# The second feed-forward product of a transformer block by Strassen's seven block products in seven of eight groups, with the gate product and the weight sums on GpSimd

## The chip, the cores and the metric

The kernel runs on one core of a Trainium2 chip. The core has five engines that run beside each other and meet at semaphores: TensorE (PE in the profile; its weight loads are PEld), VectorE (DVE), ScalarE (ACT), GpSimd (POOL) and SyncE (SP), which issues most of the DMAs. Operands lie in SBUF, products of TensorE land in eight PSUM banks of 128 x 512 float32. The metric is the device time of one execution in microseconds (us); the median of three runs of the kernel before is 1342.85 us.

## The reference, cut to what matters

One layer of a hybrid block on 512 latent tokens of width 1024. The part that matters here is its end, the feed-forward network of hidden width 4096, its gate and the final norm:

```python
def _ffn(h, w1, w2):
    return jnp.square(jax.nn.relu(h @ w1)) @ w2
...
xl = xl + ga2_l * _ffn(_modulate(_rmsnorm(xl, norm2_g[l]), sh2_l, sc2_l), w_ff1[l], w_ff2[l])
...
return _rmsnorm(xl, final_g)
```

Everything is float32. `h @ w1` is 512 x 1024 by 1024 x 4096, the second product 512 x 4096 by 4096 x 1024.

## The kernel before

TensorE multiplies in a rounded float32 type (`F32R`). To keep precision every operand is split into a rounded part and a remainder, hi and lo, and every product is three matmuls, hi·hi, hi·lo and lo·hi (`mm3`, L105 to L108). A split is a ScalarE cast (hi) and a VectorE subtraction (lo): `split` (L110 to L112) for activations, `wpiece` (L91 to L103) for a 128 x 1024 piece of weights, which it also loads over SP's queue into one of three buffers (`wraw`).

The feed-forward part begins at L911. Its 4096 hidden units are 32 tiles of 128, in eight groups of four. For a group g:

- `w1load` loads and splits the four pieces of w1 (L918), `ff1` multiplies them with the normed activations `h2T` (24 matmuls of 128 x 128 by 128 x 512 a tile, L942), and ScalarE and VectorE make relu, square and split of the result (L944 to L947): the tile `fT`, hidden units by tokens.
- `w2load` loads the four pieces of w2 (L955), VectorE multiplies them by the gate row `ga2` (L956), ScalarE casts (L958), VectorE subtracts (L963).
- `ff2` multiplies: for each of four token tiles t and two column halves n, four hidden tiles by three matmuls go into one PSUM bank (L977), and VectorE adds the bank to the residual `x1[t]` (L978). In the last group the final norm and the output follow (L979 to L998).

The loop at L1001 issues `ff1(g)`, then `ff2(g-1)`, so TensorE always has a group's product in hand whose operands are a whole stage old. The gate row `ga2` is made by `row` (L772): a transpose on TensorE, a copy, a write to memory and a broadcast read of 128 x 1024.

The framework's scheduler sets the order on each engine when the program is built; each engine then works its list strictly in that order. A tile's buffer is given out again once its last reader is done, and a DMA that waits for a buffer holds up the rest of SP's list.

Of the kernel before, what the change touches and what calls it, by code (L numbers as in the profile page):

```python
# [13 lines left out]
P = 128  # L14
# [33 lines left out]
def block(ctx, tc, a, out):  # L48
# [622 lines left out]
    with ExitStack() as fs:  # L671
# [184 lines left out]
        def last_part(t, between=None):  # L856
            tt = slice(t * P, (t + 1) * P)
            for n in range(2):
                nn = slice(n * 512, (n + 1) * 512)
                for k in range(NP1, KT):  # L860
                    w = ws[k]
                    mm3(po[2 * t + n], (yT[k][:, 0, tt], yT[k][:, 1, tt]), (w[0][:, 0, nn], w[1][:, 0, nn]),
                        False, k == KT - 1)
                nc.vector.tensor_tensor(out=x1[t][:, nn], in0=po[2 * t + n], in1=x1[t][:, nn], op=ALU.add)
                nc.scalar.activation(out=po[2 * t + n], in_=x1[t][:, nn], func=AF.Square, scale=1.0 / 32.0,
                                     accum_out=sqs[t][:, n:n + 1])
                if n == 0 and between:
# [47 lines left out]
        def w1load(g):  # L915
            r = []
            for i in range(4):
                w = wpiece(a["w1"][4 * g + i], (KT, P))  # L918
                r.append([[w[p_][:, k, :] for k in range(KT)] for p_ in range(2)])
                mod(tlast[0])  # L920
            return r

        def ff1(g, ws):
            r = []
            pfs = []
            if g == 0:
# [8 lines left out]
            for i in range(4):
                w = ws[i]
                if g == 0:
                    pf = pfs[i]
                else:
                    pf = bank("pf")  # L940
                    for k in range(KT):
                        mm3(pf, (w[0][k], w[1][k]), (h2T[:, 0, k, :], h2T[:, 1, k, :]), k == 0, k == KT - 1)  # L942
                rl = t2("rl")
                nc.scalar.activation(out=rl, in_=pf, func=AF.Relu)  # L944
                nc.scalar.activation(out=rl, in_=rl, func=AF.Square)
                ft = h6([P, 2, T], F32R, "fT") if g % 2 == 0 else m4([P, 2, T], F32R, "fT")
# [4 lines left out]
        def w2load(g):  # L951
            r = []
            for i in range(4):
                raw = wraw("w2raw")
                nc.sync.dma_start(out=raw, in_=a["w2"][4 * g + i])  # L955
                nc.vector.tensor_tensor(out=raw, in0=raw, in1=ga2, op=ALU.mult)  # L956
                hi = m4([P, D], F32R, "w2h")
                nc.scalar.copy(out=hi, in_=raw)  # L958
                lo = []
                for n in range(2):  # L960
                    nn = slice(n * 512, (n + 1) * 512)
                    l_ = s2("w2l", F32R)
                    nc.vector.tensor_tensor(out=l_, in0=raw[:, nn], in1=hi[:, nn].bitcast(F32), op=ALU.subtract)  # L963
                    lo.append(l_)
                r.append((hi, lo))
            return r

        def ff2(g, ft, w2):
            for t in range(NT):
                tt = slice(t * P, (t + 1) * P)  # L970
                if g == NG - 1:
                    sq = m2p.tile([P, 4], F32, tag="ss", name="ss")
                for n in range(2):
                    nn = slice(n * 512, (n + 1) * 512)
                    pf = bank("pf2")
                    for i in range(4):
                        mm3(pf, (ft[i][:, 0, tt], ft[i][:, 1, tt]), (w2[i][0][:, nn], w2[i][1][n]), i == 0, i == 3)  # L977
                    nc.vector.tensor_tensor(out=x1[t][:, nn], in0=pf, in1=x1[t][:, nn], op=ALU.add)  # L978
# [9 lines left out]
                if g == NG - 1:
                    nc.scalar.activation(out=sq[:, 3:4], in_=sq[:, 1:2], func=AF.Sqrt, bias=sq[:, 2:3])
                    nc.vector.reciprocal(out=sq[:, 3:4], in_=sq[:, 3:4])  # L990
                    for n in range(2):
                        nn = slice(n * 512, (n + 1) * 512)
                        if n:
                            nc.scalar.activation(out=xo[:, nn], in_=xo[:, nn], func=AF.Copy, scale=sq[:, 3:4])
                        else:
                            nc.vector.tensor_scalar(out=xo[:, nn], in0=xo[:, nn], scalar1=sq[:, 3:4],
                                                    scalar2=None, op0=ALU.mult)
                        (nc.scalar if n else nc.sync).dma_start(out=out[t * P:(t + 1) * P, nn], in_=xo[:, nn])  # L998

        prev = None  # L1000
        for g in range(NG):  # L1001
            ft = ff1(g, w1)
            m_ = mlast[0]
            if g + 1 < NG:
                w1 = w1load(g + 1)
            if g == 0:
                ga2 = row(modc[:, 5, :], m1p.tile([P, D], F32, tag="r2", name="ga2"), m_)
            if prev is not None:
                ff2(*prev)
            w2 = w2load(g)  # L1010
            prev = (g, ft, w2)
        ff2(*prev)


def _layout(np, i):
# [43 lines left out]
    d["w2"] = x(f["w_ff2"][0].reshape(NFF, P, D))  # L1059
# [32 lines left out]
```

## Time and profile before

| what | value |
|---|---|
| three runs: lowest, median, highest | 1342.56, 1342.85, 1344.24 us |
| the profiled execution: time, span | 1341.42, 1339.7 us |
| granted TensorE clock | 0.999 |
| DMA over the span | 176.35 MB, mean 132 GB/s |
| feed-forward groups 1 to 7 in the trace | from about 1006 us to the end |

A page of the profile gives busy time by engine and groups instructions by line, engine and shape. A matmul's listed duration (about 390 ns) covers its whole way through the array; the next begins long before it ends, so the distance between starts is what counts. The windows view gives each engine's busy time in a stretch; the timeline gives starts and durations in order of time. "<-" ahead of an engine names what ended the idle time before an instruction.

### The profile page before, as it was taken

To read this page: it belongs to the slowest core of one execution; us is meant where nothing else is said; L and a number is where in the kernel's file an instruction comes from. 1 tells how busy PE (TensorE), PEld (TensorE's weight loads), DVE (VectorE), ACT (ScalarE), POOL (GpSimd) and SP (SyncE) were. 2 spreads that over 40 slices of the span, in tenths; PEclk is the share of its full clock that TensorE was granted. 3 is DMA by queue.
4 is the path that set the end of the run, shared out by engine and by line. 5 is a ranking of instruction groups with operands and counts; after the bars stand their busy time and mean duration, and the time that the engine had idled before them with its cause. 6 is when DMAs were issued, how large, how long until landed. Compare 5 with 4: busy or idle time off the path is not lost. (4 is left out here: it accounts for less than half of the span.)

```text
span 1339.7 us, 16566 instructions
## 1 busy us (share of the span) xinstructions
PE 1314.7 (98%) x6214; PEld 1095.2 (82%) x6214; DVE 949.5 (71%) x1480; ACT 591.1 (44%) x857; POOL 64.0 (5%) x223
## 2 busy tenths in 40 slices
PE   6999999999999999999999999999999999999997
PEld 4778888888888888888888878888898888888886
DVE  6777968599987796777998458866577454554536
ACT  4548663346362364523646255322345332342224
POOL 2000000000010000000000010100010000000000
PEclk9999999999999999999999999999999999999999
DMA  9794332322332223322234468865534321333102
GB/s 352 281 337 134 105 105 92 65 78 95 96 117 77 65 79 105 114 74 63 87 96 138 134 207 272 300 193 189 188 111 142 110 93 52 122 110 109 65 32 79
DMA packets 84068, 176.35 MB, mean 132 GB/s; under 512 B 31730, under 2 KB 38034, under 8 KB 83987
## 3 DMA queue, kind: packets, MB, share of 16 engines
q1 hardware_dynamic: 78802, 157.46, 36.5%
q0 software_dynamic: 4608, 16.78, 3.8%
q8 instruction: 49, 0.80, 0.3%
q10 hardware_dynamic: 576, 1.05, 0.2%
q14 instruction: 33, 0.26, 0.1%
HBM read 163.25 MB, written 12.01 MB: 131 GB/s over the span
## 5 line engine op out<-in xcount | busy, mean ns | idle before, releaser
L100 ACT CAST whi<-wraw 128x1024 fp32r<-128x1024 f32 (+1 forms) x159 | 164.6, 1039 | 295.1 <-PE pv L108 76.6
L101 DVE TENSOR_TENSOR wlo<-wraw,whi 128x1024 fp32r<-128x1024 f32 (+1 forms) x159 | 191.7, 1207 | 72.0 <-ACT whi L100 70.6
L433 DVE SCALAR_TENSOR_TENSOR ca<-up,col,ca 128x512 f32<-128x512 f32 x240 | 179.6, 749 | 4.8
L393 DVE SCALAR_TENSOR_TENSOR cacc<-craw,col,cacc 128x512 f32<-128x512 f32 (+1 forms) x128 | 111.5, 879 | 2.4 <-ACT cacc L391 1.8
L958 ACT CAST w2h<-w2raw 128x1024 fp32r<-128x1024 f32 x32 | 32.3, 1053 | 154.1 <-PE pf L108 124.3
L107 PE MATMUL pf<-w2l,fT 128*128 128x512 f32 x256 | 99.6, 390 | 0.0
L108 PE MATMUL pf<-w2h,fT 128*128 128x512 f32 x256 | 99.5, 389 | 0.0
L106 PE MATMUL pf<-w2h,fT 128*128 128x512 f32 x256 | 99.2, 390 | 0.0
L978 DVE TENSOR_TENSOR x<-pf,x 128x512 f32<-128x512 f32 x64 | 44.1, 689 | 66.8 <-PE pf L108 66.5
L106 PE MATMUL pf<-h2T,whi 128*128 128x512 f32 x224 | 87.2, 389 | 0.0
L107 PE MATMUL pf<-h2T,whi 128*128 128x512 f32 x224 | 87.1, 389 | 0.0
L108 PE MATMUL pf<-h2T,wlo 128*128 128x512 f32 x224 | 87.1, 389 | 0.0
L106 PE MATMUL pv<-whi,hT 128*128 128x512 f32 x192 | 75.1, 391 | 0.0
L108 PE MATMUL pv<-whi,hT 128*128 128x512 f32 x192 | 74.7, 389 | 0.0
L107 PE MATMUL pv<-wlo,hT 128*128 128x512 f32 x192 | 74.7, 389 | 0.0
L956 DVE TENSOR_TENSOR w2raw<-w2raw,ga 128x1024 f32<-128x1024 f32 x32 | 39.0, 1224 | 45.2 <-DMA w2raw<-in_w 42.2
L107 PEld LDWEIGHTS pf<-w2l,fT 128*128 128x128 f32 x256 | 48.1, 188 | 10.6 <-DVE w2l L963 0.7
L106 PEld LDWEIGHTS pf<-w2h,fT 128*128 128x128 f32 x256 | 48.0, 188 | 10.4 <-ACT w2h L958 0.4
L108 PEld LDWEIGHTS pf<-w2h,fT 128*128 128x128 f32 x256 | 48.1, 188 | 9.7
L963 DVE TENSOR_TENSOR w2l<-w2raw,w2h 128x512 fp32r<-128x512 f32 x64 | 40.5, 685 | 15.6 <-ACT w2h L958 14.5
L106 PE MATMUL pg<-hT,whi 128*128 128x512 f32 x128 | 50.5, 394 | 0.0
L106 PE MATMUL pq<-hT,whi 128*128 128x512 f32 x128 | 50.1, 392 | 0.0
(362 smaller groups left out, 3315.9 us busy)
## 6 DMA issues: line engine op xcount, KB each, us to landing
wm<-in_wmt SPq DMA_DIRECT2D x32, 512.0 KB, 5.7
wmt<-in_wmt POOLq DMA_DIRECT2D x32, 512.0 KB, 4.6
wraw<-in_wqk SPq DMA_DIRECT2D x32, 512.0 KB, 3.5
wraw<-in_w SPq DMA_DIRECT2D x32, 512.0 KB, 4.3
w2raw<-in_w SPq DMA_DIRECT2D x32, 512.0 KB, 3.6
wraw<-in_wp SPq DMA_DIRECT2D x16, 512.0 KB, 3.5
wraw<-in_wglu SPq DMA_DIRECT2D x16, 512.0 KB, 3.6
wraw<-in_wv SPq DMA_DIRECT2D x16, 512.0 KB, 3.6
```

The costliest lines, as they stand in the source:

```text
L100: pin("act", lambda: nc.scalar.copy(out=hi[:, s], in_=raw[:, s]))
L101: wlast[0] = pin("dve", lambda: nc.vector.tensor_tensor(out=lo[:, s], in0=raw[:, s], in1=hi[:, s].bitcast(F32), op=ALU.subtract))
L106: mm(dst, lhsT=l[0], rhs=r[0], start=start, stop=False)
L107: mm(dst, lhsT=l[0], rhs=r[1], start=False, stop=False)
L108: mlast[0] = mm(dst, lhsT=l[1], rhs=r[0], start=False, stop=stop)
L393: nc.vector.scalar_tensor_tensor(out=acc[:, :n], in0=raw[:, d:d + n], scalar=ccol(wc + d), in1=acc[:, :n], op0=ALU.mult, op1=ALU.add)
L433: nc.vector.scalar_tensor_tensor(out=accv, in0=up[:, :, d:d + 64], scalar=w_, in1=accv, op0=ALU.mult, op1=ALU.add)
L956: nc.vector.tensor_tensor(out=raw, in0=raw, in1=ga2, op=ALU.mult)
L958: nc.scalar.copy(out=hi, in_=raw)
L963: nc.vector.tensor_tensor(out=l_, in0=raw[:, nn], in1=hi[:, nn].bitcast(F32), op=ALU.subtract)
L978: nc.vector.tensor_tensor(out=x1[t][:, nn], in0=pf, in1=x1[t][:, nn], op=ALU.add)
```

## The change

Groups 0 to 6 compute the second product by Strassen's scheme in Winograd's form. A group's product is cut into 2 x 2 blocks: tokens in two halves of 256, hidden units in two halves of 256 (`kh`), columns in two halves of 512 (`nh`). Seven block products a, b, e, d, f, c, g stand in place of eight; each is two token tiles by two hidden tiles by three matmuls, 12 matmuls, so a group has 84 in place of 96. What it takes in exchange:

- `aside` makes seven 128 x 256 pieces of each pair of hidden tiles (a pair p is two tiles, one of each half; group g has the pairs 2g and 2g+1): four sums and differences on VectorE, then seven splits.
- `raws` loads the four blocks of w2 as 128 x 1024 tiles, and GpSimd multiplies them by `ga2` (eight products of 128 x 512) and adds them: R, P, and in `bside` Q and S (four sums of 128 x 1024). Each of the seven operands is split as before. P is written over B12, Q over B11, S over B21.
- `ff2step` runs one block product and puts its two banks away: a, c, d and f go to eight accumulators `facc`, the rest straight into `x1`. `together` adds the accumulators to `x1` after group 6, half of it on GpSimd.
- group 7 keeps the plain product (`plain`, `ff2last`), and w1 comes in pairs (`w1pair`, `ff1pair`, banks of the other four).

`x1` becomes three tiles of three half rows, filled by eight DMAs of 128 x 512; w2 is laid out by blocks on the host.

```diff
+        def aside(p, pf):
+            f1, f2 = t2("rl"), pf[1]
+            nc.scalar.activation(out=f1, in_=pf[0], func=AF.Square)
+            nc.scalar.activation(out=f2, in_=f2, func=AF.Square)
...
+            def piece(nm, src):
+                x_ = s2("fA", F32R)
+                split(x_[:, :H2], x_[:, H2:], src)
+                A[nm] = (x_[:, :H2], x_[:, H2:])
+            sa, sb = t2("sa"), pf[0]
+            piece("a", f1[:, :H2])
+            piece("b", f2[:, :H2])
+            tt_(out=sa[:, :H2], in0=f2[:, H2:], in1=f1[:, H2:], op=ALU.subtract)
+            st_(out=sa[:, H2:], in0=sa[:, :H2], scalar=-1.0, in1=f1[:, :H2], op0=ALU.mult, op1=ALU.subtract)
+            st_(out=sb[:, H2:], in0=sa[:, H2:], scalar=-1.0, in1=f2[:, :H2], op0=ALU.mult, op1=ALU.subtract)
+            tt_(out=sb[:, :H2], in0=f1[:, :H2], in1=f1[:, H2:], op=ALU.subtract)
+            piece("e", sb[:, H2:])
+            piece("d", sa[:, :H2])
+            piece("f", sb[:, :H2])
+            piece("c", sa[:, H2:])
+            piece("g", f2[:, H2:])
...
+        ORDER = (("a", "B11"), ("b", "B21"), ("e", "B22"), ("d", "P"), ("f", "R"), ("c", "Q"), ("g", "S"))
+        pool = nc.gpsimd.tensor_tensor
+        def raws(g):
...
+            for nm, tag, kh, nh in (("B11", "wm", 0, 0), ("B21", "h", 1, 0), ("B22", "h", 1, 1), ("B12", "wm", 0, 1)):
+                b_ = rtile("r" + nm, tag)
+                nc.sync.dma_start(out=b_, in_=a["w2"][g, kh, nh])
+                for i in range(2):
+                    pool(out=b_[:, i, :], in0=b_[:, i, :], in1=ga2[:, nh * 512:(nh + 1) * 512], op=ALU.mult)
+                r[nm] = b_
+            if not last:
+                r["R"] = rtile("rR", "wraw")
+                pool(out=r["R"], in0=r["B12"], in1=r["B22"], op=ALU.add)
+                r["P"] = r["B12"]
+                pool(out=r["P"], in0=r["B11"], in1=r["B12"], op=ALU.add)
...
+        def bside(g, o):
...
+            if nm == "P":
+                r["Q"] = r["B11"]
+                pool(out=r["Q"], in0=r["P"], in1=r["B22"], op=ALU.add)
+                r["S"] = r["B21"]
+                pool(out=r["S"], in0=r["Q"], in1=r["B21"], op=ALU.add)
+            hi, lo = m4([P, 2, T], F32R, "w2h"), m4([P, 2, T], F32R, "w2l")
+            split(hi, lo, r[nm])
...
+        def ff2step(g, o):
+            s_ = ORDER[o][0]
+            hi, lo = Bop.pop((g, o))
+            for t in range(2):
+                pf = bank("pf2")
+                for i in range(2):
+                    A = As[2 * g + i][s_]
+                    tt = slice(t * P, (t + 1) * P)
+                    mm3(pf, (A[0][:, tt], A[1][:, tt]), (hi[:, i, :], lo[:, i, :]), i == 0, i == 1)
+                if s_ in "acdf":
+                    x_ = acc[s_, t]
+                    if g == 0:
+                        nc.scalar.copy(out=x_, in_=pf)
+                    else:
+                        tt_(out=x_, in0=pf, in1=x_, op=ALU.add)
...
+        for g in range(NG - 1):
+            As[2 * g + 2] = ff1pair(2 * g + 2, W.pop(2 * g + 2), lambda: opening(g))
+            if 2 * g + 4 < NPAIR:
+                W[2 * g + 4] = w1pair(2 * g + 4)
+            if g == NG - 2:
+                As[2 * g + 3] = ff1pair(2 * g + 3, W.pop(2 * g + 3))
+                R[g + 1] = raws(g + 1)
+            for o in range(7):
+                ff2step(g, o)
+                if o + 4 < 7:
+                    bside(g, o + 4)
+                elif g == NG - 2:
+                    bside(g + 1, o - 3)
+                if o == 2 and g < NG - 2:
+                    R[g + 1] = raws(g + 1)
+            if g < NG - 2:
+                As[2 * g + 3] = ff1pair(2 * g + 3, W.pop(2 * g + 3))
...
+        together()
+        ff2last(NG - 1)
```

What the scheduler makes of it, at three places. First GpSimd. In the program before, its list ends with the statistics of the second norm and the last two loads of modulation weights, and nothing of it stands in the groups:

```order
L82 TENSOR_TENSOR ss1_8001<-ss1_8001,nhalf_74 128x1
L81 TENSOR_SCALAR ss2_8002<-ss2_8002 128x1
L82 TENSOR_TENSOR ss2_8002<-ss2_8002,nhalf_74 128x1
L81 TENSOR_SCALAR ss3_8003<-ss3_8003 128x1
L82 TENSOR_TENSOR ss3_8003<-ss3_8003,nhalf_74 128x1
L711 DMA wmt_8433<-in_wmt 128x1024
L711 DMA wmt_8442<-in_wmt 128x1024
```

In the program with the change the list goes on with this round, here group 1's, once for each of the groups 0 to 6 (the number behind a name tells buffers apart):

```order
L1022 TENSOR_TENSOR rB21_8705<-rB21_8705,ga2_8500 128x512 x2
L1022 TENSOR_TENSOR rB11_8701<-rB11_8701,ga2_8500 128x512 x2
L1022 TENSOR_TENSOR rB22_8709<-rB22_8709,ga2_8500 128x512 x2
L1022 TENSOR_TENSOR rB12_8713<-rB12_8713,ga2_8500 128x512 x2
L1026 TENSOR_TENSOR rR_8717<-rB12_8713,rB22_8709 128x1024
L1028 TENSOR_TENSOR rB12_8713<-rB11_8701,rB12_8713 128x1024
L1039 TENSOR_TENSOR rB11_8701<-rB12_8713,rB22_8709 128x1024
L1041 TENSOR_TENSOR rB21_8705<-rB11_8701,rB21_8705 128x1024
```

The eight gate products moved here from VectorE, and the four sums are new; from group 2 on B12 comes ahead of B22.

Second, SP's list of loads in a middle group, before, with the semaphores that each load waits for:

```order
L955 DMA w2raw_9059<-in_w2 128x1024 [waits DMAHW7_49,DMAHW2_49,DVE_49]
L955 DMA w2raw_9068<-in_w2 128x1024 [waits DMAHW3_49,DMAHW0_49,DVE_49]
L955 DMA w2raw_9077<-in_w2 128x1024 [waits DMAHW4_49,DMAHW1_49,DVE_49]
L955 DMA w2raw_9086<-in_w2 128x1024 [waits DMAHW5_49,DVE_49,Activation_49]
L97 DMA wraw_9219<-in_w1 128x1024 [waits DVE_49,Activation_49]
L97 DMA wraw_9225<-in_w1 128x1024 [waits DVE_49,Activation_49]
```

and with the change:

```order
L1020 DMA rB21_9399<-in_w2 128x1024 [waits DMAHW2_49,DMAHW7_49,DVE_49,Pool_49]
L1020 DMA rB11_9395<-in_w2 128x1024 [waits DMAHW3_49,DVE_49]
L97 DMA wraw_9323<-in_w1 128x1024 [waits DMAHW4_49,DMAHW0_49,DVE_49]
L97 DMA wraw_9329<-in_w1 128x1024 [waits DMAHW1_49,DVE_49]
L1020 DMA rB12_9407<-in_w2 128x1024 [waits DVE_49,DMAHW6_49,Activation_49,Pool_49]
L1020 DMA rB22_9403<-in_w2 128x1024 [waits DVE_49]
L97 DMA wraw_9559<-in_w1 128x1024 [waits DMAHW5_49]
```

The load of B21 now waits for the buffer of the group before's B22, that is for its last reader, the sum Q on GpSimd; B11 waits for VectorE's split of P, B12 for that of Q, and B22 for that of S.

Third, VectorE at the start of a group's second product, before:

```order
L978 TENSOR_TENSOR x1_7789<-pf2_9257,x1_7789 128x512
L956 TENSOR_TENSOR w2raw_9373<-w2raw_9373,ga2_8459 128x1024
L978 TENSOR_TENSOR x1_7791<-pf2_9271,x1_7791 128x512
L978 TENSOR_TENSOR x1_7791<-pf2_9285,x1_7791 128x512
L978 TENSOR_TENSOR x1_7793<-pf2_9299,x1_7793 128x512
L978 TENSOR_TENSOR x1_7793<-pf2_9313,x1_7793 128x512
```

and with the change:

```order
L101 TENSOR_TENSOR wlo_9331<-wraw_9329,whi_9330 128x1024
L1067 TENSOR_TENSOR facc_8535<-pf2_9335,facc_8535 128x512
L112 TENSOR_TENSOR fA_9301<-pf_9268,fA_9301 128x256
L957 TENSOR_TENSOR sa_9297<-pf_9268,rl_9294 128x256
L1067 TENSOR_TENSOR facc_8535<-pf2_9343,facc_8535 128x512
L958 SCALAR_TENSOR_TENSOR sa_9297<-sa_9297,rl_9294 128x256
L112 TENSOR_TENSOR w2l_9352<-rR_9064,w2h_9351 128x1024
L959 SCALAR_TENSOR_TENSOR pf_9232<-sa_9297,pf_9268 128x256
L1070 TENSOR_TENSOR x1_7789<-x1_7789,pf2_9355 128x512
L960 TENSOR_TENSOR pf_9232<-rl_9294 128x256
L1070 TENSOR_TENSOR x1_7789<-x1_7789,pf2_9363 128x512
```

Between the sums that empty the banks there now stand the pieces of the next pair and the splits of R, Q and S.

TensorE's list is 84 instructions shorter (6063 and 5979 rows of the list). In a middle group it reads: steps a, b, e, d (48 matmuls), 3 of the next w1 pair, steps f, c, g (36), 93 of w1.

More of the change, by code (lines that the diff above doesn't have):

```diff
@@ new lines, in plain, with ff1pair @@
+        def plain(p, pf):
+            r = []
+            for b_ in pf:
+                rl = t2("rl")
+                nc.scalar.activation(out=rl, in_=b_, func=AF.Square)
+                ft = wp.tile([P, 2, T], F32R, tag="whi", name="fT")
+                split(ft[:, 0, :], ft[:, 1, :], rl)
+                r.append(ft)
+            return r
+        def ff1pair(p, ws, between=None):
+            pf = []
+            for i in range(2):
+                b_ = bank_a("pf")
+                for k in range(KT):
+                    mm3(b_, (ws[i][0][k], ws[i][1][k]), (h2T[:, 0, k, :], h2T[:, 1, k, :]), k == 0, k == KT - 1)
+                relu_(b_)
+                pf.append(b_)
+                if i == 0 and between:
+                    between()
+            return (plain if p >= NPAIR - 2 else aside)(p, pf)
@@ L929, in ff1, with ff1first @@
+        def ff1first(ws):
+            pf = [bank("pf") for _ in range(4)]
+            for o, n in ((0, 256), (256, 256)):
                 for i in range(4):
                     for k in range(KT):
-                        mm3(pfs[i][:, o:o + n], (ws[i][0][k], ws[i][1][k]),
+                        mm3(pf[i][:, o:o + n], (ws[i][0][k], ws[i][1][k]),
                             (h2T[:, 0, k, o:o + n], h2T[:, 1, k, o:o + n]), k == 0, k == KT - 1)
@@ L934, in ff1 @@
                         rest(i)
[L935 to L938, printed above, removed]
-                else:
[L940 to L946, printed above, removed]
-                split(ft[:, 0, :], ft[:, 1, :], rl)
-                r.append(ft)
@@ L949, in ff1 @@
-            return r
[L951 to L966, printed above, removed]
@@ new lines, in block @@
+        Bop = {}
+        def bside(g, o):
+            r = R[g]
+            nm = ("B11", "B21", "B12", "B22")[o] if g == NG - 1 else ORDER[o][1]
+            if nm == "P":
[5 more added lines that the diff above has]
+            split(hi, lo, r[nm])
+            Bop[g, o] = (hi, lo)
@@ new lines, in together @@
+        def together():
+            for t in range(2):
+                A_, C_, D_, F_ = (acc[s_, t] for s_ in "acdf")
+                tt_(out=x1(t, 0), in0=x1(t, 0), in1=A_, op=ALU.add)
+                tt_(out=C_, in0=C_, in1=A_, op=ALU.add)
+                tt_(out=A_, in0=D_, in1=C_, op=ALU.add)
+                tt_(out=x1(t, 1), in0=x1(t, 1), in1=A_, op=ALU.subtract)
+            for t in range(2):
+                A_, C_, D_, F_ = (acc[s_, t] for s_ in "acdf")
+                pool(out=x1(2 + t, 0), in0=x1(2 + t, 0), in1=C_, op=ALU.add)
+                pool(out=x1(2 + t, 0), in0=x1(2 + t, 0), in1=F_, op=ALU.add)
+                pool(out=x1(2 + t, 1), in0=x1(2 + t, 1), in1=A_, op=ALU.subtract)
+                pool(out=x1(2 + t, 1), in0=x1(2 + t, 1), in1=F_, op=ALU.subtract)
@@ L988, in ff2 @@
[L988 to L1012, printed above, removed]
+                    for m in range(4):
+                        i, kh = m % 2, m // 2
+                        f_ = As[2 * g + i][kh]
+                        hi, lo = Bop[g, 2 * n + kh]
+                        mm3(pf, (f_[:, 0, tt], f_[:, 1, tt]), (hi[:, i, :], lo[:, i, :]), m == 0, m == 3)
```

110 lines of the change are left out of this document (78 added, 32 removed).

## The prediction

> **What bounds the kernel now.** I read the page first: TensorE is busy almost throughout, the others have room, GpSimd has next to nothing.
>
> ```profile
> PE 1314.7 (98%) x6214; PEld 1095.2 (82%) x6214; DVE 949.5 (71%) x1480; ACT 591.1 (44%) x857; POOL 64.0 (5%) x223
> ```
>
> Then the stage, in the windows view: two groups' time in the feed-forward part, each as long as one group (below).
>
> ```profile
> core 0: us, PE busy (x) PEld busy (x) DVE busy (x) ACT busy (x) POOL busy (x), PEclk, DMA share, GB/s
> 1079.20:1122.70 43.50, 43.50 (x194) 36.03 (x193) 22.60 (x28) 14.99 (x20) 0.00 (x0) 1.00 0.30 97
> 1122.70:1166.20 43.50, 43.50 (x194) 36.03 (x193) 21.97 (x28) 15.10 (x20) 0.00 (x0) 1.00 0.31 97
> ```
>
> TensorE is busy for all of 43.5 us, VectorE for 22 to 23, ScalarE for 15, GpSimd for none, at the full clock. The waits of TensorE's weight loads from 1000 us to the end are two rows of 1.1 us together, so no other engine holds TensorE back; fewer matmuls there are time saved, one for one, until something else is late.
>
> ```profile
> PEld pf L107 <- DVE w2l L963: 0.7, 3, 0.2
> PEld pf L106 <- ACT w2h L958: 0.4, 1, 0.4
> ```
>
> What a matmul is worth is the distance between banks that are emptied, each after 12 matmuls:
>
> ```profile
> 1125.49 0.69 DVE L978 TENSOR_TENSOR x<-pf,x 128x512 f32<-128x512 f32 x1 [2.03 <-PE pf L108]
> ...
> 1133.64 0.69 DVE L978 TENSOR_TENSOR x<-pf,x 128x512 f32<-128x512 f32 x1 [2.03 <-PE pf L108]
> ```
>
> Three distances are 8.15 us, so 12 matmuls take 2.72 us and one 0.2264 us (not the 390 ns listed). A group of 192 takes 43.5 us.
>
> **What the change removes.** Seven groups lose 12 matmuls each: 84 x 0.2264 = **19.0 us**, and a middle group needs TensorE for 180 x 0.2264 = 40.75 us. This is the most that can be won, but for the 1.1 us of waits above.
>
> **What it adds on ScalarE and VectorE.** The prices:
>
> ```profile
> L101 DVE TENSOR_TENSOR wlo<-wraw,whi 128x1024 fp32r<-128x1024 f32 x30 | 36.6, 1221 | 15.9 <-ACT whi L100 15.4
> L978 DVE TENSOR_TENSOR x<-pf,x 128x512 f32<-128x512 f32 x64 | 44.1, 689 | 66.8 <-PE pf L108 66.5
> L243 DVE TENSOR_TENSOR hT<-hf,hT 128x256 fp32r<-128x256 f32 x8 | 3.4, 422 | 2.4 <-ACT hT L242 2.4
> L958 ACT CAST w2h<-w2raw 128x1024 fp32r<-128x1024 f32 x32 | 32.3, 1053 | 154.1 <-PE pf L108 124.3
> L945 ACT ACTIVATE rl<-rl 128x512 f32<-128x512 f32 x32 | 20.2, 632 | 0.8
> L944 ACT ACTIVATE rl<-pf 128x512 f32<-128x512 f32 x32 | 19.0, 592 | 22.1 <-PE pf L108 22.1
> ```
>
> One behind the other on VectorE, starts lie closer than durations:
>
> ```profile
> 1109.47 1.23 DVE L956 TENSOR_TENSOR w2raw<-w2raw,ga 128x1024 f32<-128x1024 f32 x1 [2.38 <-DMA w2raw<-in_w]
> 1110.61 1.22 DVE L101 TENSOR_TENSOR wlo<-wraw,whi 128x1024 fp32r<-128x1024 f32 x1
> ...
> 1117.77 0.68 DVE L112 TENSOR_TENSOR fT<-rl,fT 128x512 fp32r<-128x512 f32 x1
> 1118.38 0.68 DVE L978 TENSOR_TENSOR x<-pf,x 128x512 f32<-128x512 f32 x1
> ```
>
> ```profile
> 371.12 0.42 DVE L551 SCALAR_TENSOR_TENSOR E<-spc,E 128x256 f32<-128x256 f32 x1
> 371.47 0.08 DVE L551 DVE_READ_ACCUMULATOR E<-spc,E 128x1 f32 x1
> 371.47 0.75 DVE L433 SCALAR_TENSOR_TENSOR ca<-up,col,ca 128x512 f32<-128x512 f32 x1
> ```
>
> So 1024 columns count 1.14 us, 512 columns 0.61, 256 columns 0.35 (0.42 where the next needs the result). VectorE per middle group: 14 banks x 0.61 = 8.5; 7 splits of weight sums and 4 of w1 x 1.14 = 12.5; 14 pieces x 0.35 = 4.9; 8 sums x 0.42 = 3.4; together 29.3 us, against 22 to 23 before. ScalarE: 11 casts of 1.05, four relus of 0.59, four squares of 0.63 and 14 casts of 256 columns at some 0.4 (1053 ns less three quarters of its columns) are 22 us. Both fit into 40.75 us. The tightest place is the banks: step f begins 51 matmuls, 11.5 us, after step a and writes the bank that VectorE frees last in step e. Its list up to there is three splits of 1024, five banks, six pieces and four sums, 3.4 + 3.05 + 2.1 + 1.7 = 10.2 us, and it begins one cast (1.05 us) after step a. So this costs nothing, with 0.3 us to spare; if VectorE comes later, TensorE waits for as much.
>
> **What it adds on GpSimd.** The trace holds no product or sum of that size there. The nearest rows:
>
> ```profile
> L546 POOL TENSOR_SCALAR_AFFINE_SELECT E<-E x32: 293/295/1091, 160.4 to 720.5; 128x128 f32<-128x128 f32 x32
> L77 POOL TENSOR_SCALAR sq<-sq 128x1 f32<-128x1 f32 x16 | 3.1, 192 | 56.0 <-ACT hm L621 55.9
> ```
>
> Alone, a select over 128 columns takes 295 ns, an instruction with one column 192. The difference over 128 is 0.80 ns per column read. From below: inputs read together, 0.19 + 0.80 x 512 = 0.60 us for a gate product and 1.01 for a sum of 1024. From above: all of the 295 ns counts per column, 2.3 ns, which gives 1.18 and 2.36. I take two inputs one after the other, 1.6 ns: **1.02 and 1.84**, as the price of a read is in both rows and the second read costs as the first. Eight products and four sums are 15.5 us per group (8.8 to 18.9), which would be hidden many times over if GpSimd worked beside VectorE. It does not always:
>
> ```profile
> 389.40 1.23 DVE L101 TENSOR_TENSOR wlo<-wraw,whi 128x1024 fp32r<-128x1024 f32 x1 [0.66 <-ACT whi L100]
> 389.69 1.09 POOL L546 TENSOR_SCALAR_AFFINE_SELECT E<-E 128x128 f32<-128x128 f32 x1 [2.93 <-DMA E<-Hd]
> ```
>
> ```profile
> 162.42 0.42 POOL L546 TENSOR_SCALAR_AFFINE_SELECT E<-E 128x128 f32<-128x128 f32 x1 [1.73 <-DMA E<-Hd]
> 162.60 1.31 DVE L101 TENSOR_TENSOR wlo<-wraw,whi 128x1024 fp32r<-128x1024 f32 x1
> ```
>
> ```profile
> 374.34 0.29 POOL L546 TENSOR_SCALAR_AFFINE_SELECT E<-E 128x128 f32<-128x128 f32 x1 [1.25 <-DMA E<-Hd]
> 374.36 0.56 DVE L112 TENSOR_TENSOR ptl<-tp,pth 128x384 fp32r<-128x384 f32 x1
> ```
>
> The select that met a split with two operands in SBUF took 1.09 us and ended 0.15 us after it; its own work is some 0.1, so 0.05 is the hand-over. The split that met a select was 0.09 us late. Beside a split with one operand in PSUM the select took its 0.29. So one of the two stands still while the other reads. The Trainium skill says the same (SBUF — State Buffer, § Who interferes with whom): a VectorE instruction with two SBUF inputs and a GpSimd instruction that reads SBUF exclude each other, and the loser blocks entirely. By that rule the sum is the one worked out here; without it the change would be the first rival. The trace agrees, with its 1.09 us, as far as GpSimd loses; for a long GpSimd sum ahead of a split no run here shows it.
>
> **The loop that this closes.** Buffers tie each group to the one before: B22 is loaded into the buffer of S, so after S is split. From there, S to S:
>
> ```profile
> w2raw<-in_w SPq DMA_DIRECT2D x23, 512.0 KB, 3.6
> ```
>
> 1. The load: 3.6 us.
> 2. GpSimd: two products, R, P. Three splits of VectorE get between (B11's rest 0.6, B21 and B22 1.1 each): 2.8 us.
> 3. P is split; Q and S hold up that split and the next one; then the four gate products of the next B21 and B11 arrive and alternate with the splits of the pieces. So six products and four sums lie in the loop in all.
> 4. VectorE's list from P to S: 8 of 1024, 6 banks, 14 pieces, 8 sums = 9.1 + 3.7 + 4.9 + 3.4 = 21.1 us; some 1.5 us of it have a PSUM operand and run beside GpSimd, and some 2 us are waits for ScalarE's casts: 21.6.
>
> Without GpSimd that is 28.0 us. With it 28.0 + 6 x 1.02 + 4 x 1.84 + 10 x 0.05 = **42.0 us**, above TensorE's 40.75. (Bounds: 36.1, where TensorE sets the pace, and 45.0.) Behind VectorE's waiting split stand the pieces and the bank sums, and TensorE waits for these at step f. Behind ScalarE's cast of P stand the next w1 cast and the relu of the pair that the next group needs. On SP two loads of w1 stand behind those of B21 and B11; their casts come two tiles of w1 (10.9 us) after their buffers are free, against 3.6 for a load, so they cost nothing.
>
> The loop does not hold everywhere. From step f of group 0 to that of group 1 TensorE has 169 matmuls, in the next four stretches 180 each, and into group 6 225 (51 us, pair 15 is put ahead). The first five are 889 matmuls, 201.3 us; at the loop's pace 5 x 42.0 = 210.0. So **8.7 us** go back (none at the lower bound, 23.7 at the upper).
>
> **The ends.** Group 0 waits for the gate row:
>
> ```profile
> 1005.67 0.60 ACT L944 ACTIVATE rl<-pf 128x512 f32<-128x512 f32 x1 [0.96 <-PE pf L108]
> 1007.65 0.33 SPq L780 DMA_DIRECT2D ga<-rowd  x1
> 1011.27 3.50 DVE L956 TENSOR_TENSOR w2raw<-w2raw,ga 128x1024 f32<-128x1024 f32 x3 [2.96 <-DMA ga<-rowd]
> ```
>
> It was there 5.6 us after the first stage's last relu began. Now a square and a piece's cast stand ahead of its copy, so about 6.9; two products, cast and split (2.0 + 1.1 + 1.1) make 11.1 against the 10.9 us of the w1 pair that covers it, and P's chain (ten GpSimd instructions, 11.8 us, then 2.2) is done 20.9 us after the start, and step d wants it at 21.8 (10.9, three steps of 2.72 and 12 matmuls between). With VectorE's locks I put **3 us** here (0 to 5). At the end `together` is 8 sums of 0.61 us on VectorE and 8 of 1.02 on GpSimd, beside group 7's 96 matmuls (21.7 us), which need VectorE for two instructions of 0.61 every 2.72 us: nothing, and up to 3 us if that cover falls short. The halved loads of `x1` and the two early loads of w2 lie where SP's list waited for buffers: nothing.
>
> **The sum.** The profiled execution took 1341.42 us, 1.4 below the median of the runs. 1341.4 - 19.0 + 8.7 + 3 = 1334.1; on the median's footing **1335.5 us**.
>
> **The rivals.**
> - TensorE stays the bound: the sums read both inputs at once, or hold the port for a part of their time only. For it speaks that the select held a split up by 0.09 us and not by its whole 0.42. Then 1341.4 - 19.0 + 1 + 1.4 = **1325**.
> - GpSimd's instructions cost the upper bound, 1.18 and 2.36. The place is Q and S ahead of the splits behind P; the loop is 45.0 us, 23.7 go back, and 1341.4 - 19.0 + 23.7 + 3 + 1.4 = **1350.5, slower**. It decides from a loop of 43.5 us, that is at about 1.1 and 2.1. For it speaks that a select is a simpler instruction than a sum. Against it, that 192 ns of the 295 are there with a single column. The Trainium skill has a price for this place (GPSIMD Engine Reference, § Performance versus the Vector engine): 4497 ns for a sum of 2048 float32 columns, 1.96 times VectorE's; estimated from it the products are 1.2 and the sums 2.3 us, the loop 44.9, and the time 1350; no run here shows it.
> - Both meet: a loop of 43 to 43.6 us gives everything back, **1342**, no change.
>
> **How the numbers follow.** TensorE bound 0.22 (1323 to 1329); my forecast, part given back, 0.33 (1329 to 1340); all given back 0.13; slower by the loop 0.32 (1345.6 to 1360). A measurement of this kernel can tell about 0.2%, 2.7 us, from no change. So faster 0.55, same 0.13, slower 0.32. The range 1323 to 1354 leaves out the longest loops, and covers both ends of GpSimd's price; the forecast's own range is 1329 to 1340.
>
> **What would show it.** In the profile after: gate products near 1.02 us and sums near 1.84 where no split meets them; distances of middle groups near 42 us, TensorE idle by one or two us a group, its waits on VectorE's bank sums at step f; VectorE's 128 x 1024 splits listed longer than 1.22 us where a sum was ahead. TensorE without waits and groups of 40.75 us would show the first rival, groups over 43.5 us the second. I am wrong in kind if TensorE waits elsewhere: for a load, for ScalarE, or in group 0 for much over 5 us.

## The result and the profile after

The changed kernel takes **1360.43 us** (median of 4 runs, 1360.14 to 1361.48) against 1342.70 before (4 runs): the ratio is 1.0135, with a 95% interval of 1.0123 to 1.0147. It is slower by 1.3%, and outside the range that was given. The profiled execution took 1360.71 us, its span is 1358.9 us, 19.2 us longer than before (1339.7), although TensorE has 84 matmuls and so 19.0 us less to do. **38.2 us** have to be found.

The page of the changed kernel, busy time by engine and the granted clock in 40 slices:

```profile
PE 1305.3 (96%) x6130; PEld 1081.2 (80%) x6130; DVE 1056.5 (78%) x1605; ACT 629.5 (46%) x956; POOL 264.5 (19%) x323
...
PEclk9999999999999999999999999999997999999999
```

TensorE is busy for 96% instead of 98%, GpSimd for 264.5 us instead of 64.0, and in one slice the clock is not full. The windows view (columns as in the prediction) shows where: a stretch of group 0, then a middle group.

```profile
1030.00:1040.00 10.00, 4.85 (x13) 3.85 (x14) 5.36 (x3) 5.31 (x6) 9.76 (x5) 0.66 0.15 46
1040.00:1050.00 10.00, 3.18 (x11) 2.32 (x10) 10.00 (x12) 1.63 (x5) 10.00 (x6) 0.81 0.14 59
1050.00:1060.00 10.00, 10.00 (x39) 8.10 (x39) 7.89 (x6) 6.43 (x9) 4.94 (x4) 0.85 0.42 159
...
1163.90:1207.80 43.90, 41.68 (x181) 33.56 (x180) 37.29 (x48) 19.77 (x33) 25.18 (x13) 1.00 0.30 96
```

From 1030 to 1050 TensorE is busy for 8.0 of 20 us and GpSimd for nearly all of them, and behind the waits the clock drops. In the middle a group takes 43.9 us, more than the 43.5 of before, with TensorE busy for 41.7; VectorE went from 22 to 37 us. What TensorE's matmuls waited for (us in total, times, longest), first in group 0, then from 1060 us on:

```profile
PE pf L106 <- DVE x L1070: 6.8, 1, 6.8
PE pf L106 <- ACT facc L1065: 6.6, 2, 6.2
PE pf L107 <- DVE w2l L112: 1.2, 2, 0.7
PE pf L106 <- ACT w2h L111: 0.9, 1, 0.9
```

```profile
PE pf L106 <- DVE x L1070: 6.7, 10, 0.7
PE pf L106 <- DVE facc L1067: 3.5, 4, 0.9
```

That is 25.7 us in 20 waits: 15.5 in six of group 0 and 10.2 in 14 later ones. All but 2.1 us of it end with VectorE's bank sums, or with ScalarE's copies of banks in group 0. A wait costs a little more than it is listed with (timeline of TensorE: start, duration, line, in brackets the listed wait):

```profile
1216.19 0.39 PE L108 MATMUL pf<-w2h,fA 128*128 128x512 f32 x1
1217.44 0.50 PE L106 MATMUL pf<-w2h,fA 128*128 128x512 f32 x1 [0.87 <-DVE facc L1067]
1217.78 0.40 PE L107 MATMUL pf<-w2l,fA 128*128 128x512 f32 x1
```

From one start to the next 1.25 us pass instead of 0.23, which is 1.02 and not 0.87, and the first matmul then takes 0.34 instead of 0.23. So 20 waits cost 25.7 + 20 x 0.27 = 31.1 us. The account of the 38.2:

| where | us |
|---|---|
| group 0: six waits (15.5 + 1.6) | 17.1 |
| group 0: half clock behind its two long waits | 4.4 |
| groups 1 to 5: 14 waits (10.2 + 3.8) | 14.0 |
| stage begins later (first transposes at 987.0, before 985.5) | 1.5 |
| tail (last matmul starts 8.6 us before the end, before 7.4) | 1.2 |

The 4.4 us of the clock are half of the time in which matmuls ran at half speed: 4.2 us behind the first long wait (1035.15 to 1039.31, where the clock rose again) and 4.7 behind the second (1048.28 to 1052.97). What the last two rows come from was not taken apart.

### The profile page after: what moved, and what is told of

The parts are those of the page before. It is cut to its first block, busy times and chain, and to the rows that moved or that the text cites. A ratio compares the mean times of both kernels' runs of the same rounds, so it can differ in the third digit from the quotient of the medians.

```text
span 1358.9 us, 16826 instructions
## 1 busy us (share of the span) xinstructions
PE 1305.3 (96%) x6130; PEld 1081.2 (80%) x6130; DVE 1056.5 (78%) x1605; ACT 629.5 (46%) x956; POOL 264.5 (19%) x323
## 5 line engine op out<-in xcount | busy, mean ns | idle before, releaser
L100 ACT CAST whi<-wraw 128x1024 fp32r<-128x1024 f32 (+1 forms) x159 | 164.4, 1039 | 259.7 <-PE pv L108 75.7
L101 DVE TENSOR_TENSOR wlo<-wraw,whi 128x1024 fp32r<-128x1024 f32 (+1 forms) x159 | 213.4, 1343 | 67.9 <-ACT whi L100 67.2
L1022 POOL TENSOR_TENSOR rB<-rB,ga 128x512 f32<-128x512 f32 x64 | 108.0, 1715 | 120.0 <-DMA rB<-in_w 79.0
L112 DVE TENSOR_TENSOR w2l<-rB,w2h 128x1024 fp32r<-128x1024 f32 x46 | 77.4, 1683 | 41.2 <-ACT w2h L111 41.1
L106 PE MATMUL pf<-w2h,fA 128*128 128x512 f32 x196 | 79.4, 406 | 24.6 <-DVE x L1070 13.5
L111 ACT CAST w2h<-rB 128x1024 fp32r<-128x1024 f32 x46 | 48.0, 1054 | 98.0 <-POOL rB L1028 34.5
L107 PE MATMUL pf<-w2l,fA 128*128 128x512 f32 x196 | 77.9, 397 | 1.2 <-DVE w2l L112 1.2
L108 PE MATMUL pf<-w2h,fA 128*128 128x512 f32 x196 | 77.5, 396 | 0.0
L106 PEld LDWEIGHTS pf<-w2h,fA 128*128 128x128 f32 x196 | 37.5, 192 | 39.3 <-DVE x L1070 12.4
L711 POOL DMA_DIRECT2D wmt<-in_wmt x32 | 17.5, 547 | 188.1 <-DVE wmt L719 179.7
L111 ACT CAST fA<-pf 128x256 fp32r<-128x256 f32 x56 | 21.0, 374 | 64.7 <-DVE pf L960 58.4
L106 PE MATMUL p<-whi,hT 128*128 128x512 f32 x128 | 50.0, 391 | 0.8 <-ACT zm L366 0.8
```

Of the source, the lines that this page charges most:

```text
L100: pin("act", lambda: nc.scalar.copy(out=hi[:, s], in_=raw[:, s]))
L101: wlast[0] = pin("dve", lambda: nc.vector.tensor_tensor(out=lo[:, s], in0=raw[:, s], in1=hi[:, s].bitcast(F32), op=ALU.subtract))
L106: mm(dst, lhsT=l[0], rhs=r[0], start=start, stop=False)
L107: mm(dst, lhsT=l[0], rhs=r[1], start=False, stop=False)
L108: mlast[0] = mm(dst, lhsT=l[1], rhs=r[0], start=False, stop=stop)
L111: nc.scalar.copy(out=hi, in_=src)
```

## The experiments

Two theories stood against each other. **G**: GpSimd is at fault, by its price (a product 1.25 us, a sum 2.40, where nothing is in the way) and because its instructions and VectorE's splits exclude each other. **V**: VectorE's own new list is too long or lies wrong, and GpSimd has little to do with it. The prices come from the profile after; the three numbers behind the count are the shortest, the median and the longest duration of a line's instructions, in ns:

```profile
L1022 POOL TENSOR_TENSOR rB<-rB,ga x64: 1254/1476/2287, 1015.6 to 1305.5; 128x512 f32<-128x512 f32 x64
```

```profile
L1039 POOL TENSOR_TENSOR rB<-rB,rB x7: 2362/2408/2412, 1033.6 to 1284.9; 128x1024 f32<-128x1024 f32 x7
```

A sum takes 2.40 us alone (line 1039) and 3.26 where a split came between (line 1028, in the turn of the loop below). The Trainium skill's price (GPSIMD Engine Reference, § Performance versus the Vector engine), 4497 ns for 2048 columns, agrees within a tenth with twice the 2.40 us, 4.80.

But for the repeat of run 1, each run is a single execution. The kernel before took 1340.27 us beside runs 1, 2, 4 and 5, and 1341.67 to 1345.69 us beside the others, so nothing is read into a difference of less than some 3 us.

### 1. Everything on VectorE

```diff
-        pool = nc.gpsimd.tensor_tensor
+        pool = nc.vector.tensor_tensor
```

This takes in the eight sums of `together`.

> All gate products and weight sums go to VectorE; GpSimd does nothing in the stage. Theory G (GpSimd's instructions are dear, 1.25 us a product and 2.40 us a sum alone, and VectorE's splits and they exclude each other): the two long waits of group 0 (6.4 and 7.0 us) fall below 3 us together, the clock stays at full speed, a split takes 1.22 us again, and VectorE has 29.3 + 8 x 0.61 + 4 x 1.14 = 38.7 us of work in a group of 40.75; 1330 to 1342 us. Rival V (VectorE's own new list is too long or lies wrong, GpSimd apart): 9.4 us more on VectorE make it worse, groups of 44 us or more and at least 1358 us.

Measured: 1325.05 us in a single run, 5 us below the range of G. It was timed again:

> The kernel with all products and sums on VectorE again, timed in rounds: 1324 to 1327 us against 1340 to 1343 before, a ratio of 0.986 to 0.990. If its single run was a stray, it lies above 1335.

Five runs: median **1323.83 us** (1322.46 to 1324.24) against 1343.25 before, ratio 0.9848 (0.9835 to 0.9862), just below what was expected. A middle group of this kernel in the windows view, and the groups of its products and splits:

```profile
1100.00:1140.75 40.75, 40.75 (x182) 33.73 (x181) 39.58 (x61) 19.47 (x33) 0.00 (x0) 1.00 0.35 115
```

```profile
L112 DVE TENSOR_TENSOR w2l<-rB,w2h 128x1024 fp32r<-128x1024 f32 x46 | 55.4, 1215 | 0.2 <-ACT w2h L111 0.2
...
L1022 DVE TENSOR_TENSOR rB<-rB,ga 128x512 f32<-128x512 f32 x64 | 40.7, 681 | 3.0 <-DMA rB<-in_w 2.3 <-DMA ga<-rowd 0.2
```

TensorE has no wait left in the loop, a group takes its 40.75 us, and VectorE is busy for 39.6 of them. A split takes 1.22 us, where the changed kernel has 1.68. So V has fallen: 9.4 us more work per group on VectorE made the kernel 36.6 us faster. The gain over before, 19.4 us, is about the 19.0 us of the 84 matmuls.

### 2 and 3. One half on VectorE

Run 2 has the sums on VectorE (P, Q and S like R):

```diff
-                pool(out=r["R"], in0=r["B12"], in1=r["B22"], op=ALU.add)
+                tt_(out=r["R"], in0=r["B12"], in1=r["B22"], op=ALU.add)
```

> Only the four weight sums of a group go to VectorE, the eight gate products stay on GpSimd. G: the loop from S to S is 28.0 + 6 x 1.25 + 4 x 1.19 = 40.3 us, so groups of 40.75 to 41.5 us instead of 43.9; in group 0, P is ready some 5 us earlier, its first long wait shrinks to 1.5 us, the second goes; 1330 to 1337 us. V: groups stay at 43.9 us or grow, 1350 us or more.

Measured 1339.67 us, 2.7 above the range of G. The middle groups came out as expected: three of them from one S sum to the next took 122.4 us, 40.8 each, without a wait.

```profile
1103.70:1226.10 122.40, 122.40 (x541) 101.36 (x540) 107.88 (x154) 61.28 (x100) 38.12 (x24) 1.00 0.30 104
```

What was missed is group 0: its longest wait was 4.4 us, not 1.5, since the eight products ahead of P take some 13 us on GpSimd, with VectorE's splits between them.

Run 3 has the products there:

```diff
-                    pool(out=b_[:, i, :], in0=b_[:, i, :], in1=ga2[:, nh * 512:(nh + 1) * 512], op=ALU.mult)
+                    tt_(out=b_[:, i, :], in0=b_[:, i, :], in1=ga2[:, nh * 512:(nh + 1) * 512], op=ALU.mult)
```

> Only the eight gate products of a group go to VectorE, the four weight sums stay on GpSimd (the other half of the run with the sums on VectorE). If the two halves add up, 1360.7 - (1339.7 - 1325.1) = 1346 us. If the loop decides, 28.0 + 6 x 0.61 + 4 x 2.45 = 41.5 us and more where a sum holds a split up, groups of 41.5 to 42.5 us; with the products of group 0 done in 4.9 us instead of 13.0 its first long wait goes and part of the second stays: 1338 to 1346 us. Rival: the sums alone make the loop and group 0, then 1352 us or more.

Measured 1355.09 us; the rival held. Two middle groups took 87.5 us, 43.75 each, with 3.6 us of TensorE idle:

```profile
1144.00:1231.50 87.50, 83.93 (x362) 66.96 (x361) 80.38 (x111) 39.74 (x67) 24.40 (x8) 1.00 0.28 96
```

The forecast loop of 41.5 us left out that every sum now meets a split or a product of VectorE: R took 2.86 us on average instead of 2.40, and a split 2.03 instead of 1.22. With nothing on GpSimd the time is 1323.8, with the products alone 1339.7, with the sums alone 1355.1, with both 1360.4. The halves don't add up (15.9 and 31.3 against 36.6), so a part of what each costs is covered by the other; no run takes this apart.

### 4. Group 0 on VectorE

```diff
-                    pool(out=b_[:, i, :], in0=b_[:, i, :], in1=ga2[:, nh * 512:(nh + 1) * 512], op=ALU.mult)
+                    (tt_ if g == 0 else pool)(out=b_[:, i, :], in0=b_[:, i, :], in1=ga2[:, nh * 512:(nh + 1) * 512], op=ALU.mult)
...
-                pool(out=r["R"], in0=r["B12"], in1=r["B22"], op=ALU.add)
+                (tt_ if g == 0 else pool)(out=r["R"], in0=r["B12"], in1=r["B22"], op=ALU.add)
```

> The products and two of the sums (R and P) of group 0 alone go to VectorE, everything else stays as in the changed kernel. G: group 0 loses its long waits and the half clock (13 to 18 us), the middle groups keep 43.9 us: 1343 to 1348 us. Rival R (group 0 is late because the gate row arrives late, not because of GpSimd): the waits stay for the most part, 1354 us or more.

The edit moved all four sums of group 0 (P, Q and S like R), which the expectation has wrong. Measured 1349.44 us, 11.0 less than the changed kernel and 1.4 above the range of G; the gate row as the cause (R) fell. Not all of the loss went, because some of it moved: the next group's products now begin while VectorE is still in the list of group 0, and its sums follow at 1049 us. Where TensorE's matmuls waited longest in this kernel:

```profile
PE pf L106 <- DVE facc L1067: 8.0, 5, 4.9
PE pf L106 <- ACT fA L111: 4.0, 1, 4.0
```

Two waits are long, 4.0 us in group 0 and 4.9 in group 1, and behind both the clock was halved. The expectation that group 0 would lose its long waits was a miss.

### 5. Without the sums

```diff
-                r["R"] = rtile("rR", "wraw")
-                pool(out=r["R"], in0=r["B12"], in1=r["B22"], op=ALU.add)
+                r["R"] = r["B22"]
...
-                pool(out=r["P"], in0=r["B11"], in1=r["B12"], op=ALU.add)
-                pool(out=r["Q"], in0=r["P"], in1=r["B22"], op=ALU.add)
-                pool(out=r["S"], in0=r["Q"], in1=r["B21"], op=ALU.add)
```

> The four weight sums of a group are left out: the splits read B22, B12, B11 and B21 in place of R, P, Q and S, so the output is not the reference's; matmuls, splits, loads and gate products are as in the changed kernel. G: the loop loses 4 x 2.4 to 3.3 us, 10 to 11 us in all, and TensorE sets the pace: groups of 40.75 us, and little waiting in group 0; 1325 to 1332 us. V: VectorE's list is unchanged, so TensorE still waits at the bank sums: groups over 42.5 us and 1345 us or more.

Without the sums this kernel does not compute the product; its time is what matters here. Measured 1338.43 us, between the two ranges. Four middle groups took 165 us, 41.3 each:

```profile
1081.50:1246.50 165.00, 163.81 (x719) 134.34 (x717) 123.01 (x187) 81.56 (x132) 53.20 (x34) 1.00 0.33 100
```

TensorE is idle for 0.3 us in each: V's 42.5 fell, and with the products alone on GpSimd a group is half a microsecond longer than TensorE's 40.75. The rest is group 0 again, as in run 2 (eight products in a row on GpSimd, 9.7 us of waits by the distances of the starts, and 3.4 us at half clock). The kernel with the sums on VectorE (run 2) took 1.2 us more than this one, which two single runs cannot tell apart.

### 6. Sums that nobody waits for

Is it GpSimd's slowness as a link of the chain, or the exclusion by itself? Here the chain is that of run 1, and GpSimd only repeats sums.

```diff
+        scr = m3p.tile([P, 2, T], F32, tag="r1", name="scr")
+        def again(x, y):
+            nc.gpsimd.tensor_tensor(out=scr, in0=x, in1=y, op=ALU.add)
...
+                again(r["R"], r["B22"])
...
+                again(r["P"], r["B22"])
```

> All products and sums on VectorE as in the run with everything there (1325.05 us), and GpSimd adds four pairs of the same tiles per group into a tile that nobody reads (the load of the last row of gains moves behind the loop to make room for that tile). Nothing waits for these sums but the next loads into the tiles that they read. Theory G1 (the exclusion itself costs: a split that comes while a sum runs stands still for the sum's rest): splits of up to 3.4 us, VectorE's 38.7 us of work grow by 6 to 9 us, groups of 43 to 47 us, 1338 to 1360 us. Theory G2 (only GpSimd's slowness costs, as a link of the chain from load to split; VectorE loses no more than 0.1 us an instruction): groups of 40.75 to 41 us, 1325 to 1328 us.

Measured 1364.59 us, **40.8 us more than run 1** for 28 sums, 1.5 us each, and above even the range of G1. One such sum on GpSimd and what VectorE did beside it, in the timeline of each engine:

```profile
1188.87 2.40 POOL L1007 TENSOR_TENSOR scr<-rR,rB 128x1024 f32<-128x1024 f32 x1 [24.74 <-DVE rR L1028]
```

```profile
1189.26 3.10 DVE L1031 TENSOR_TENSOR rB<-rB,rB 128x1024 f32<-128x1024 f32 x1
```

GpSimd's sum ends at 1191.27, 2.01 us after VectorE's sum was issued; VectorE's took 3.10 us instead of 1.21, 1.89 more. It stood still for the rest of the sum, which no run had shown when the prediction was made. Over the whole execution VectorE's busy time grew by 45.4 us with the same number of instructions (the pages of run 1's repeat and of this run):

```profile
PE 1295.3 (98%) x6130; PEld 1078.8 (82%) x6130; DVE 1062.9 (80%) x1705; ACT 628.4 (48%) x956; POOL 63.8 (5%) x223
PE 1308.3 (96%) x6130; PEld 1085.0 (80%) x6130; DVE 1108.3 (81%) x1705; ACT 627.9 (46%) x956; POOL 146.9 (11%) x251
```

For TensorE, by the distances of the starts, this is some 32 us of waits and 9 us of half clock behind the longer ones. In the windows view VectorE is full, by hold-ups that are listed as busy time:

```profile
1168.70:1212.90 44.20, 41.60 (x182) 33.48 (x180) 43.44 (x59) 17.86 (x31) 11.68 (x4) 1.00 0.30 96
```

VectorE is busy for 43.4 of 44.2 us, with work for 39.6. Waits of VectorE for loads are 4.9 us in all, so the loads into the tiles that GpSimd reads explain little. The exclusion alone is enough to lose more than Strassen's form wins.

### 7. A buffer for B22

```diff
-            for nm, tag, kh, nh in (("B11", "wm", 0, 0), ("B21", "h", 1, 0), ("B22", "h", 1, 1), ("B12", "wm", 0, 1)):
+            for nm, tag, kh, nh in (("B11", "wm", 0, 0), ("B21", "h", 1, 0), ("B22", "b22", 1, 1), ("B12", "wm", 0, 1)):
...
+                if tag == "b22":
+                    return m3p.tile([P, 2, T], F32, tag="r1", name=nm)
```

> The changed kernel with a buffer of its own for B22, so that its load no longer waits for the split of S (the load of the last row of gains moves behind the loop to make room). If the loop from S to S paces the middle groups, it now closes over B12, whose buffer is free after Q's split, 3.3 us earlier: groups of 40.75 to 41.5 us instead of 43.9, group 0 as late as before, 1346 to 1350 us. Rival (VectorE with its splits held up is full, the loop is none): groups stay at 43.9 us, 1358 to 1362 us.

Measured 1352.33 us, 8.1 less than the changed kernel. The group is what the loop theory said, 41.0 us with TensorE always busy:

```profile
1115.55:1156.55 41.00, 41.00 (x181) 33.70 (x180) 39.74 (x48) 20.16 (x34) 25.91 (x12) 1.00 0.30 103
```

The total is 2.3 us above the range, and the stage began 3.9 us later in this run than in the profile of the changed kernel (991 against 987 us). TensorE had waited 2.1 us for VectorE at 848 us, ahead of the feed-forward part, and the clock was at half from 851 to 855 us, as in no other run; what made VectorE late there stays open.

### 8. Both repairs

The edits of runs 4 and 7 together:

```diff
-                    pool(out=b_[:, i, :], in0=b_[:, i, :], in1=ga2[:, nh * 512:(nh + 1) * 512], op=ALU.mult)
+                    (tt_ if g == 0 else pool)(out=b_[:, i, :], in0=b_[:, i, :], in1=ga2[:, nh * 512:(nh + 1) * 512], op=ALU.mult)
...
+                if tag == "b22":
+                    return m3p.tile([P, 2, T], F32, tag="r1", name=nm)
```

> Both repairs at once: the products and all four sums of group 0 on VectorE, and a buffer of its own for B22; GpSimd still makes the products and sums of groups 1 to 6. If group 0 and the loop are two separate losses, the gains add: 1360.4 - 11.0 (group 0 on VectorE) - 8.1 (own buffer, as its run came out) = 1341 us, or 1337 if the late start of that run was chance. If they are one loss that only moves (VectorE held up by GpSimd's next group), no more than the larger of the two is won: 1347 us or more.

Measured 1340.79 us: the gains add, so group 0 and the loop are two losses. Even so repaired, with GpSimd still at work in six groups, the kernel gains nothing that can be told from before; run 1 is 17 us faster.

## Why the prediction was wrong

The profiled execution was forecast at 1334.1 us and took 1360.71, 26.6 more. Of these, 18.5 us are group 0 (3 forecast, 21.5 lost), 5.3 the loop (8.7 forecast, 14.0 lost), and 2.7 the tail and the earlier stages, which were put at nothing. The terms that failed are the first two, and the price of GpSimd's instructions and the exclusion stand behind both.

**Right: what could be won.** 84 matmuls of 0.2264 us, 19.0 us, and TensorE as the bound of the stage without GpSimd. Run 1 won 19.4 us and shows groups of 40.75 us. The first rival's 1325 us is the time of run 1 to about 1 us, but not for the rival's reason: in run 1 GpSimd has nothing to do in the loop, and where the two do meet they stop each other in full (run 6). Right too were the places: ScalarE and VectorE have room for Strassen's own work, no matmul waits for a load, and in the middle groups TensorE waits for VectorE's bank sums alone.

**Right in kind, short in size: the loop.** It was put at 42.0 us, and came out at 43.9 from group 1 to group 6, in five stretches. One turn of it in the changed kernel, in the timelines of VectorE, GpSimd and ScalarE, from one split of S (the first row) to the next (the last):

```profile
1138.09 1.22 DVE L112 TENSOR_TENSOR w2l<-rB,w2h 128x1024 fp32r<-128x1024 f32 x1
```

```profile
1143.00 4.34 POOL L1022 TENSOR_TENSOR rB<-rB,ga 128x512 f32<-128x512 f32 x2 [0.61 <-DMA rB<-in_w]
1147.42 2.40 POOL L1026 TENSOR_TENSOR rR<-rB,rB 128x1024 f32<-128x1024 f32 x1
1149.90 3.26 POOL L1028 TENSOR_TENSOR rB<-rB,rB 128x1024 f32<-128x1024 f32 x1
```

```profile
1153.19 1.05 ACT L111 CAST w2h<-rB 128x1024 fp32r<-128x1024 f32 x1 [4.77 <-POOL rB L1028]
```

```profile
1154.28 2.45 DVE L112 TENSOR_TENSOR w2l<-rB,w2h 128x1024 fp32r<-128x1024 f32 x1 [3.38 <-ACT w2h L111]
...
1182.00 1.22 DVE L112 TENSOR_TENSOR w2l<-rB,w2h 128x1024 fp32r<-128x1024 f32 x1
```

S is split by 1139.31; B22 lands and its product starts 3.7 us later (forecast 3.6); products, R and P take 10.2 us (forecast 8.7); the cast 1.1 and VectorE's list from P's split to the end of S's 28.9, together 30.0 (forecast 29.7). The step that failed is the **price of GpSimd's instructions**, "1.02 and 1.84", chosen inside bounds of 1.18 and 2.36 above. Measured are 1.25 and 2.40, just over the upper bound: 2.25 ns a column and some 0.1 us besides. The price came out low because only 103 of the select's 295 ns were put down to its columns; how much of the select's 295 ns goes by the column no run shows, so that the upper bound came so near is in part luck. Two more errors of the sum work the other way. With the measured prices its formula gives 28.0 + 6 x 1.25 + 4 x 2.40 + 0.5 = 45.6 us and not 43.9, so GpSimd's whole time in VectorE's list is 1.7 us too much. And the loop did not hold in the first of the five stretches that the prediction counts: from group 0 to group 1 the sum S came 31.9 us later. Five turns of 43.9 would give back 18.2 us, and 14.0 were lost. Run 7 shows that this is a loop: a buffer more, and the groups take 41.0 us.

**Wrong: group 0.** "With VectorE's locks I put 3 us here (0 to 5)"; 21.5 us were lost there (17.1 and 4.4). This is the larger part of the error, and by the prediction's own sign ("in group 0 for much over 5 us") it was wrong here in kind. It has three pieces. First, P came late. It was to be ready 11.8 us after the gate row, and it took 17.9 (products 13.0, R and P 4.8). The measured prices alone make 8 x 1.25 + 2 x 2.40 = 14.8 of it; the other 3 us fell in the eight products, between which VectorE made three splits. The gate row itself came 8.0 us after the last relu of the first stage (1007.59 to 1015.64) and not 6.9. By the prediction's count P's chain then ends at 20.9 + 1.1 + 6.1 = 28.1 us, 6.3 us after step d wants it, and the first long wait is 6.2 us. Behind ScalarE's cast of P stands the copy of a bank, and TensorE waits for that:

```profile
1033.57 1.04 ACT L111 CAST w2h<-rB 128x1024 fp32r<-128x1024 f32 x1 [6.08 <-POOL rB L1028]
1034.52 0.58 ACT L1065 COPY facc<-pf 128x512 f32<-128x512 f32 x1
```

```profile
1035.15 0.79 PE L106 MATMUL pf<-w2h,fA 128*128 128x512 f32 x1 [6.19 <-ACT facc L1065]
...
1048.28 0.80 PE L106 MATMUL pf<-w2h,fA 128*128 128x512 f32 x1 [6.82 <-DVE x L1070]
```

Second, the exclusion on VectorE. Its list from P's split to the first bank sum, while GpSimd was at work without a break:

```profile
1034.64 2.41 DVE L112 TENSOR_TENSOR w2l<-rB,w2h 128x1024 fp32r<-128x1024 f32 x1 [5.72 <-ACT w2h L111]
1036.98 0.42 DVE L959 SCALAR_TENSOR_TENSOR pf<-sa,pf 128x256 f32<-128x256 f32 x1
1037.31 3.08 DVE L101 TENSOR_TENSOR wlo<-wraw,whi 128x1024 fp32r<-128x1024 f32 x1
1040.31 1.52 DVE L960 TENSOR_TENSOR pf<-rl 128x256 f32<-128x256 f32 x1
1041.74 2.28 DVE L112 TENSOR_TENSOR w2l<-rR,w2h 128x1024 fp32r<-128x1024 f32 x1
1043.94 2.28 DVE L101 TENSOR_TENSOR wlo<-wraw,whi 128x1024 fp32r<-128x1024 f32 x1
1046.14 0.41 DVE L112 TENSOR_TENSOR fA<-pf,fA 128x256 fp32r<-128x256 f32 x1
1046.48 1.15 DVE L112 TENSOR_TENSOR fA<-sa,fA 128x256 fp32r<-128x256 f32 x1
1047.55 0.68 DVE L1070 TENSOR_TENSOR x<-x,pf 128x512 f32<-128x512 f32 x1
```

At the prices of the prediction these eight instructions ahead of the bank sum are 4 x 1.14 + 4 x 0.35 = 6.0 us; they took 12.9, and the wait that ends at 1048.28 is 6.8 us long. The prediction had the exclusion, but the one row that it had for VectorE's side, a short select, cost VectorE 0.09 us. Beside a long sum the later of the two loses what is left of the earlier, 1.89 us in the pair of run 6. In the loop this was put in, as GpSimd's whole time in VectorE's list; in group 0 it was a guess. Third, the clock, which the prediction didn't have at all (4.4 us, below). Run 4 took 11.0 us of this away, and part of the rest came back a group later.

**The rivals.** The rival on the slower side named the right mechanism and nearly the right price: its condition, products at about 1.1 and sums at about 2.1 us, was met. Its 1350.5 us is 10 short, and two of its errors cancel in part. It had 23.7 us given back by a loop of 45.0, where 14.0 were, and it took over the 3 us of group 0, where 21.5 were lost. It had been given 0.32, a chance below "faster" only because the lower price was thought nearer.

## What to carry to other kernels

GpSimd's idle time is not free time for work on VectorE's kind of operands: here an addition that costs 1.14 us of VectorE's time took 2.40 us there and could stop VectorE for most of that, so ask first whether VectorE has room (here 39.6 of 40.75 us was room enough). When a price is bounded from two sides and the forecast changes sign between them, let the chances say that the price is not known, or measure it first. And work out the first turn of a pipelined loop on its own, with the engines' lists in order: there the gate row had only just come, and P's lateness went into TensorE's wait in full.

## What the runs showed of the hardware

**In these runs TensorE's clock was halved after it had stood for somewhat over half of a window of 3.41 us.** Within a run the points where the clock changes lie whole multiples of 3.41 us apart (1032.49, 1039.31, 1046.14 and 1052.97 us in the changed kernel). Two windows of that grid, each with the one behind it (busy time of TensorE first, the clock in the column behind GpSimd):

```profile
1028.09:1031.50 3.41, 1.64 (x8) 1.03 (x7) 2.14 (x4) 3.22 (x6) 3.41 (x3) 1.00 0.00 0
1031.50:1034.92 3.42, 3.42 (x9) 2.11 (x7) 3.42 (x4) 1.93 (x3) 3.42 (x3) 0.50 0.84 305
```

```profile
1125.75:1129.16 3.41, 1.67 (x7) 1.42 (x8) 3.41 (x7) 0.51 (x2) 0.00 (x0) 1.00 0.00 0
1129.16:1132.58 3.42, 3.42 (x16) 2.82 (x15) 3.42 (x9) 2.04 (x5) 0.00 (x0) 1.00 0.00 0
```

Busy for 1.64 us of a window (run 5), the clock is at half in the next; busy for 1.67 us (run 6), it stays. In the stage of eight kernels (the changed one and runs 2 to 8), each full-speed window in which TensorE stood for 1.94 us or more was followed by a halved one, 18 in all, and none in which it stood for 1.79 us or less (counted are distances of over 0.4 us between starts, less the 0.23 of a matmul). The Trainium skill gives the length of the window and the half rate (TensorE: Matmul & The Clock Gate, § Part 1: The HAM clock gate), as measured here, and in its § HAM oscillation — how this bites in real kernels it warns of pauses over some 3.4 us; these runs show that 1.9 us within one window are enough, so a wait of 2 us can cost 1.7 us more, half of a window. It need not, where it falls across two windows: in run 6 two starts at 1124 us lie 3.35 us apart, and the clock stayed full (the second pair above is the later part of this wait).
